# A decoder layer in fp32 on one core: eight modulation tiles moved into the up projection, the last pair's sums kept in SBUF, two blocks scaled by items of their own

## The chip, the core and the metric

The kernel runs on one core of one Trainium2 chip. The core has five engines that work side by side and wait for each other by semaphores: TensorE (PE, matmuls), VectorE (DVE), ScalarE (ACT), GpSimd (POOL) and SyncE (SP, which here only issues transfers). Sixteen DMA engines move data between the chip's memory (DRAM) and the on-chip memory SBUF; PE writes its results to PSUM. The metric is the time of one execution on the device in microseconds (us); a kernel's time is the median of its runs.

## The reference, cut to what matters

One decoder layer for 512 tokens of width 1024, all in fp32. A vector `c` is projected to six modulation vectors; two attention branches are gated, merged and projected; a gated MLP with a causal convolution of width 3 follows. Each half ends in a layer norm whose sum is scaled by a modulation vector.

```python
mod = c @ w_ada + b_ada                              # 6 x 1024
sh1, sc1, gt1, sh2, sc2, gt2 = split(mod, 6)
u = x * (1 + sc1) + sh1
...
merged = sigmoid(g_a) * (y_fox @ w_fox_proj) + sigmoid(g_b) * (y_sb @ w_sb_proj)
x = layer_norm(alpha * x + (1 + gt1) * (merged @ w_o), ln1_g, ln1_b)
u2 = x * (1 + sc2) + sh2
h = causal_depthwise_conv(u2 @ w_up, conv_w, conv_b)  # 5632 columns
h_gate, h_val = split(h, 2)
x = layer_norm(alpha * x + (1 + gt2) * ((silu(h_gate) * h_val) @ w_down), ln2_g, ln2_b)
```

`gt2`, the sixth vector, is needed last: it scales the output of the down projection.

## The kernel before

**Products.** Each fp32 product is made of three matmuls. A number is split into a high part (ACT copies it, rounded) and a low part (DVE subtracts, `lo_of`, L90); `mm3` (L130 to L133) and `product` (L1053 to L1055) then add high x high, high x low and low x high. So each tile of weights costs one ACT and one DVE operation before PE may use it: `wh` and `wl`.

**The ring of items.** All weights pass through one list, `items`. An item is a source and a routine that works on it. `weights(i)` loads up to item i + 5 on SP's queue into five buffers of 128x1024 (`raw`, 512 KB each) and runs the routines in the list's order. A buffer comes free when its item's routine has read it. The place of an item in the list therefore sets when it is loaded, and what it is loaded behind. SP's order is that of the list; on the other engines a scheduler sets the order.

**Modulation tiles.** The matrix of the modulation passes as 32 tiles of 128x1024 (`wa1`), beside some that are loaded ahead. Tiles 8 to 23 are for `sh2` and `sc2` (`mod_col`, one DVE operation of 128x1024 each, L194). Tiles 0 to 7 and 24 to 31 are for `gt1` and `gt2`: `ada_proc` (L566 to L580) multiplies each half by a column of `c` and adds it up in `ac`, two DVE operations per tile (L574 for a group's first, else L579). Four tiles make a group, g = 0, 1 for `gt1` and g = 6, 7 for `gt2`. `ada_split` splits a group's sum in high and low part, and `ada_sum` adds over the partitions with two matmuls against ones and puts the result into half of `gt[i]` (L600). Tiles 0 to 31 are put in the list by `add_ada`, behind projections, values and gates of the attention.

**The gates.** From about 296 to 345 us PE runs the gates of branch A (tiles of `in_wct`), the branch's projection and the merge. POOL adds the two branches (L731) and multiplies w_o's tiles by `gt1` (`wo_proc`, L625), DVE makes `ml` and `wl`. Then the output projection and the layer norm follow, up to 400.

**The up projection** runs over 44 tiles of `w_up` (n = 0 to 43), 24 matmuls of 512 columns each, from about 400 to 690; ACT and DVE do the convolution behind each tile (L1103 to L1105).

**The down projection** is in blocks of a 2 x 2 scheme with seven products (Winograd's form of Strassen's), whose weights come in 11 pairs p, each with four blocks of 512 columns: B11, B12, B22, B21. Per pair there are three items in the up projection's list: one raw item, to which POOL's queue adds a second load in memory (L156); B11, split; and `pair_proc` (L934 to L946). The last one makes two sums of blocks (L939, L940), splits them for the pair's early products, and stores for later, on ACT's queue, the raw item's two sums to `t13[p]` (L943) and B22 scaled by `gt2`, `wg` (L938), to `wgt[p]` (L944). Three of the seven products run early; the other four run after the up projection, in a phase each: phase Z (items `zi`: the right half of `t13`), W1 (`vi`: the left half of `t13`), X (`xi`: B21) and W (`wi`: `wgt`). Each of these items holds two pairs. `phase` (L1157) runs such a phase; `early_products` (L1059) runs the pairs' early products, that of the last pair, p = 10, inside phase Z. `tail` (L1142) does the layer norm by row blocks of 128 and sends them out.

## Time and profile before

| What | Value |
|---|---|
| Runs, us | 765.11, 768.05, 767.78 (median 767.78) |
| Profiled execution, us | 765.17 |
| Its span, first to last instruction, us | 763.4 |
| Mean granted clock of PE | 0.993 |
| DRAM read, written, MB | 117.07, 10.75 |

The profile is one execution. A row of a group gives the engine, the line, the operation, the tiles as out<-in, their shapes and a count; a row of the timeline starts with the start and the duration in us, and ends in brackets with the time that the engine stood idle before it and what ended that. "PEld" is the load of a matmul's stationary side, which runs beside PE. A duration of a matmul is longer than the step from one to the next, as they overlap in the array; 128x512 matmuls follow each other at 0.22 to 0.23 us.

### The profile page before, as it was taken

Reading aid. Unit: us, or ns where it says so; the run is one execution under the profiler, and the core shown is the slowest. Engines: PE = TensorE matmul, PEld = TensorE weight load, DVE = VectorE, ACT = ScalarE, POOL = GpSimd, SP = SyncE. Lnnn points to the kernel's source line nnn. Section 1 sums busy time; section 2 is a strip of 40 time slices with the busy share of each in tenths; the row PEclk is TensorE's granted clock in tenths of the full one; section 3 lists DMA queues with packets and bytes.
Section 4 is the critical chain, followed back from the end, with each engine's and each line's share of the span. In section 5 each row is a group of like instructions: output and inputs, shape, how many; then the busy total and the mean of one; then the engine's idle time right before and its main releaser. Section 6 shows DMA issues by size and latency. Waiting matters only on the chain.

```text
span 763.4 us, 9879 instructions
## 1 busy us (share of the span) xinstructions
PE 738.1 (97%) x3478; PEld 609.1 (80%) x3478; DVE 610.4 (80%) x1017; ACT 385.3 (50%) x678; POOL 107.0 (14%) x136
## 2 busy tenths in 40 slices
PE   8999999989989999899999999999999999999993
PEld 4878888877878888688889888888888888886783
DVE  6869799887699786975567989966786777768998
ACT  4567466684875664343046554443553355344630
POOL 1035223443000011363000000000000000000010
PEclk9999999999999999999999999999999999999998
DMA  9954556333344134552055576646754665555922
GB/s 334 406 186 133 170 173 214 110 112 112 114 135 139 66 128 143 175 185 78 5 190 147 166 229 193 190 156 190 263 171 161 222 192 151 169 186 159 321 81 78
DMA packets 43524, 128.54 MB, mean 168 GB/s; under 512 B 5681, under 2 KB 6193, under 8 KB 43474
## 3 DMA queue, kind: packets, MB, share of 16 engines
q1 hardware_dynamic: 37602, 112.09, 42.6%
q0 software_dynamic: 2416, 6.88, 5.0%
q10 hardware_dynamic: 3456, 8.93, 3.4%
q8 instruction: 27, 0.44, 0.2%
q14 instruction: 23, 0.19, 0.1%
HBM read 117.07 MB, written 10.75 MB: 167 GB/s over the span
## 4 chain that ended last, share of the span: by engine, by line
PE 73%; DVE 14%; DMA 5%; issue 4%; ACT 3%; SPq 1%; POOL 0%; DVEq 0%; ACTq 0%; POOLq 0%
PE ps L133 15%; PE ps L131 15%; PE ps L132 15%; PE ps L294 4%; PE ps L1054 4%; PE ps L1055 4%; PE ps L1053 4%; DVE wl L90 3%; DMA raw<-in_wa 2%; PE ps L887 2%; PE ps L886 2%; PE ps L888 2%; DVE om L506 2%; PE ps L527 1%; DVE raw L194 1%
## 5 line engine op out<-in xcount | busy, mean ns | idle before, releaser
L90 DVE TENSOR_TENSOR wl<-raw,wh 128x1024 fp32r<-128x1024 f32 (+2 forms) x114 | 136.1, 1194 | 60.2 <-ACT wh L176 60.0
L176 ACT ACTIVATE wh<-raw 128x1024 fp32r<-128x1024 f32 (+1 forms) x105 | 109.7, 1045 | 133.5 <-PE ps L132 90.4
L131 PE MATMUL ps<-u2h,wh 128*128 128x512 f32 (+1 forms) x376 | 141.5, 376 | 0.0
L133 PE MATMUL ps<-u2h,wl 128*128 128x512 f32 (+1 forms) x376 | 141.5, 376 | 0.0
L132 PE MATMUL ps<-u2l,wh 128*128 128x512 f32 (+1 forms) x376 | 141.4, 376 | 0.0
L133 PE MATMUL ps<-uh,wl 128*128 128x512 f32 x200 | 79.0, 395 | 2.7 <-DVE wl L90 2.7
L133 PEld LDWEIGHTS ps<-u2h,wl 128*128 128x128 f32 x376 | 70.8, 188 | 12.9
L131 PEld LDWEIGHTS ps<-u2h,wh 128*128 128x128 f32 x376 | 70.8, 188 | 12.8
L132 PEld LDWEIGHTS ps<-u2l,wh 128*128 128x128 f32 x376 | 70.8, 188 | 12.7
L131 PE MATMUL ps<-uh,wh 128*128 128x512 f32 x200 | 80.2, 401 | 0.0
L132 PE MATMUL ps<-ul,wh 128*128 128x512 f32 x200 | 78.9, 395 | 0.0
L156 POOL DMA_DIRECT2D raw<-in_wdp x11 | 9.5, 867 | 295.3 <-DVE raw L940 149.6
L133 PEld LDWEIGHTS ps<-uh,wl 128*128 128x128 f32 x200 | 37.9, 190 | 11.5 <-DVE wl L90 3.1
L507 POOL TENSOR_TENSOR pt<-pt,om 128x127 f32<-128x127 f32 (+3 forms) x32 | 42.7, 1347 | 9.4 <-DVE om L506 9.4
L131 PEld LDWEIGHTS ps<-uh,wh 128*128 128x128 f32 x200 | 38.0, 190 | 7.5
L132 PEld LDWEIGHTS ps<-ul,wh 128*128 128x128 f32 x200 | 38.1, 191 | 7.3
L1103 ACT ACTIVATE cv<-ps,cw 128x512 f32<-128x512 f32 x44 | 33.7, 766 | 16.8 <-PE ps L133 11.1
L1104 DVE SCALAR_TENSOR_TENSOR cv<-ps,cw,cv 128x511 f32<-128x511 f32 x44 | 32.8, 745 | 6.3 <-ACT cv L1103 6.3
L1111 ACT ACTIVATE cv<-cv 128x512 f32<-128x512 f32 x22 | 13.9, 632 | 41.7 <-DVE cv L1105 41.7
L1105 DVE SCALAR_TENSOR_TENSOR cv<-ps,cw,cv 128x510 f32<-128x510 f32 x44 | 32.7, 745 | 0.3
L625 POOL TENSOR_TENSOR raw<-raw,gt 128x1024 f32<-128x1024 f32 x8 | 20.5, 2567 | 69.7 <-DMA raw<-in_wo 58.2
L1054 PE MATMUL ps<-wl,hv 128*128 128x512 f32 x72 | 28.7, 398 | 1.4 <-DVE wl L90 1.4
(224 smaller groups left out, 1611.0 us busy)
## 6 DMA issues: line engine op xcount, KB each, us to landing
raw<-in_wup SPq DMA_DIRECT2D x44, 512.0 KB, 4.3
raw<-in_wa SPq DMA_DIRECT2D x32, 512.0 KB, 3.4
raw<-in_wct SPq DMA_DIRECT2D x25, 512.0 KB, 3.8
raw<-in_wdp SPq DMA_DIRECT2D x22, 512.0 KB, 5.6
wa<-in_wa SPq DMA_DIRECT2D x14, 512.0 KB, 7.7
raw<-in_wdp POOLq DMA_DIRECT2D x11, 512.0 KB, 7.2
raw<-in_wdp SPq DMA_DIRECT2D x22, 256.0 KB, 6.3
t<-raw ACTq DMA_DIRECT2D x11, 512.0 KB, 2.9
```

The costliest lines, as they stand in the source:

```text
L90: return V.tensor_tensor(o, i, fl(hi), ALU.subtract)
L131: PE.matmul(ps, wh, ah, start=first, stop=False)
L132: PE.matmul(ps, wh, al, start=False, stop=False)
L133: return PE.matmul(ps, wl, ah, start=False, stop=last)
L176: state["hi"] = S.activation(h[:, 0:cols], r[:, 0:cols], AF.Copy)
L294: PE.matmul(grp[g], w, u, start=j == 0 and n == 0, stop=j == KT - 1 and n == (1 if g == 7 else 2))
L507: G.tensor_tensor(pt[b][:, s : e - 1], pt[b][:, s : e - 1], om[:, s + 1 : e], ALU.mult)
L1053: PE.matmul(ps, ah, bh, start=first, stop=False)
L1054: PE.matmul(ps, ah, bl, start=False, stop=False)
L1103: S.activation(t, ps, AF.Identity, bias=cw[:, n, 3:4], scale=cw[:, n, 2:3])
L1104: V.scalar_tensor_tensor(t[:, 1:], ps[:, 0:511], cw[:, n, 1:2], t[:, 1:], ALU.mult, ALU.add)
L1105: V.scalar_tensor_tensor(t[:, 2:], ps[:, 0:510], cw[:, n, 0:1], t[:, 2:], ALU.mult, ALU.add)
```

## The change

Tiles 24 to 31 of the modulation leave the attention's part of the list and stand in that of the up projection, group 7 first. The two groups are split and summed apart. The last pair's sums are neither stored nor loaded; they are split in SBUF, so `t13` has ten tiles, and phases Z and W1 have five items and a last pair without one. Pairs 0 and 1 make no `wg`; their B22 is loaded a second time by an item of its own, scaled in place and stored by POOL's queue. The late items of `wgt` are put elsewhere in X's list.

```diff
+GTILES = (3, 5, 7, 8, 12, 16, 20, 24)
...
-            elif adas[0] < 32:
+            elif adas[0] < 24:
...
             add_bproj(1, j, lambda m, j=j: ma.__setitem__(j, m))
-            if j >= 3:
-                add_ada()
...
     for j in range(KT):
         add_bproj(0, j, merge(j))
-        add_ada()
...
-    add_ada(32 - adas[0])
+    add_ada(24 - adas[0])
...
     def pair_proc(p):
         def f(r):
             b = items[pi[p][0]][4]
-            g = z(F32, "wg")
-            V.tensor_tensor(g, r[:, 0:512], gt[1][:, 512:1024], ALU.mult)
+            if p > 1:
+                g = z(F32, "wg")
+                V.tensor_tensor(g, r[:, 0:512], gt[1][:, 512:1024], ALU.mult)
...
             with tc.issue_after(state["last"].ins):
-                S.dma_start(t13[p], b)
-                S.dma_start(wgt[p], g)
+                if p < FP - 1:
+                    S.dma_start(t13[p], b)
+                if p > 1:
+                    S.dma_start(wgt[p], g)
+            if p == FP - 1:
+                state["t13"] = wdc_proc(b)
             return w
         return f

-    wui, pi = [], []
+    def scale_proc(p):
+        def f(r):
+            V.tensor_tensor(r[:, 0:512], r[:, 0:512], gt[1][:, 512:1024], ALU.mult)
+            G.dma_start(wgt[p], r[:, 0:512])
+        return f
...
     for n in range(2 * FT):
         wui.append(add_item(wup[n], split_proc))
+        if n in GTILES:
+            k = GTILES.index(n)
+            wai[(10, 28)[k // 4]] = add_item(wa1[(28, 24)[k // 4] + k % 4], ada_proc((28, 24)[k // 4] + k % 4))
+        if n in (17, 21):
+            add_item(wdp[n // 4 - 4][:, 1024:1536], scale_proc(n // 4 - 4))
...
-    for p in range(0, FP, 2):
-        add_two(zi, lambda q: t13[q][:, 512:1024], p, FP)
+    for p in range(0, FP - 1, 2):
+        add_two(zi, lambda q: t13[q][:, 512:1024], p, FP - 1)
...
-        if p < 8:
+        if p < 10:
             add_late()
...
-            if n == 3:
-                for g in (6, 7):
-                    list(ada_split(g, 0))
-            if n == 4:
-                for g in (6, 7):
-                    list(ada_sum(g))
+            if n in (10, 28):
+                list(ada_split(7 if n == 10 else 6, wai[n]))
+            if n in (11, 30):
+                list(ada_sum(7 if n == 11 else 6))
...
-    def phase(ps, idx, end, take, mark):
+    def phase(ps, idx, end, take, mark, last=None):
...
+        if end < FP:
+            t = take(end)
+            for i in range(2):
+                product(ps[i], t[:, top[i]], t[:, bot[i]], *[v[last] for v in state["t13"]], False, True)
+            mark(len(idx))
```

How this moves instructions is seen in three places. The first is DVE at the gates, about 307 to 322 us. `sg` is a gate times a projection, `ml` the merged rows' low part, `wol` the low part of a tile of w_o, `ac` group 7's sum. Before:

```order
L90 TENSOR_TENSOR ml_3094<-sg_2919,mh_3093 128x512
L574 TENSOR_SCALAR ac_618_3108<-raw_3066,cTs 128x512
L579 SCALAR_TENSOR_TENSOR ac_618_3108<-raw_3066,cTs,ac_618_3108 128x512
L579 SCALAR_TENSOR_TENSOR ac_618_3108<-raw_3098,cTs,ac_618_3108 128x512 x2
L90 TENSOR_TENSOR wl_3183<-raw_3161,wh_3182 128x1024
L579 SCALAR_TENSOR_TENSOR ac_618_3108<-raw_3159,cTs,ac_618_3108 128x512
L619 TENSOR_TENSOR sg_2972<-ps_3139,sg_2972 128x512
L579 SCALAR_TENSOR_TENSOR ac_618_3108<-raw_3159,cTs,ac_618_3108 128x512
L579 SCALAR_TENSOR_TENSOR ac_618_3108<-raw_3163,cTs,ac_618_3108 128x512
L90 TENSOR_TENSOR ml_3155<-sg_2972,mh_3154 128x512
L579 SCALAR_TENSOR_TENSOR ac_618_3108<-raw_3163,cTs,ac_618_3108 128x512
L90 TENSOR_TENSOR wl_3254<-raw_3213,wh_3253 128x1024
```

The last row is the `wl` of 320.88. The same stretch with the change:

```order
L91 TENSOR_TENSOR ml_3074<-sg_2897,mh_3073 128x512
L91 TENSOR_TENSOR wol_3087<-raw_3044,woh_3085 128x512
L91 TENSOR_TENSOR wol_3088<-raw_3044,woh_3086 128x512
L91 TENSOR_TENSOR wl_3152<-raw_3139,wh_3151 128x1024
L620 TENSOR_TENSOR sg_2950<-ps_3119,sg_2950 128x512
L91 TENSOR_TENSOR wl_3196<-raw_3143,wh_3195 128x1024
L91 TENSOR_TENSOR ml_3135<-sg_2950,mh_3134 128x512
L91 TENSOR_TENSOR wl_3232<-raw_3184,wh_3231 128x1024
```

No `ac` is left among them. The counterpart of the row of 320.88 is `wl_3196`; it now stands ahead of the second `ml`, and the next one, `wl_3232`, follows that `ml` at once.

The second place is SP's queue at the start of phase W1, whose first item is pairs 0 and 1 (`t_0`, `t_1`). Before:

```order
L153 DMA raw_6361<-t_8_70 128x512
L153 DMA raw_6361<-t_9_71 128x512
L153 DMA raw_6378<-t_10_72 128x512
L153 DMA raw_6410<-t_0_62 128x512
L153 DMA raw_6410<-t_1_63 128x512
```

With the change:

```order
L154 DMA raw_6362<-t_8_70 128x512
L154 DMA raw_6362<-t_9_71 128x512
L154 DMA raw_6386<-t_0_62 128x512
L154 DMA raw_6386<-t_1_63 128x512
L154 DMA raw_6419<-t_2_64 128x512
```

The load of `t_10` is gone. DVE, at the same place, works on pair 10's sums as follows (`raw_6255` holds them, `wdl` are their low parts):

```order
L938 TENSOR_TENSOR raw_6255<-raw_6255,raw_6217 128x512
L91 TENSOR_TENSOR wl_6460<-raw_6386,wh_6459 128x1024
L939 TENSOR_TENSOR raw_6255<-raw_6255 128x512
L91 TENSOR_TENSOR wdl_6371<-raw_6255,wdh_6369 128x512
L91 TENSOR_TENSOR wl_6490<-raw_6419,wh_6489 128x1024
L91 TENSOR_TENSOR wdl_6372<-raw_6255,wdh_6370 128x512
L91 TENSOR_TENSOR wdl_6380<-raw_6217,wdh_6378 128x512
L91 TENSOR_TENSOR wdl_6381<-raw_6217,wdh_6379 128x512
```

Before, the two sums and the two `wdl` of `raw_6254` stood in a row, without a `wl` between them; `wl_6460` and `wl_6490` are W1's first two items.

The third place is DVE early in the up projection (n = 1 to 4), where there is now an `ac` of group 7 between the convolution's operations (`cv`):

```order
L575 TENSOR_SCALAR ac_758_4051<-raw_3841,cTs 128x512
L1124 TENSOR_TENSOR cv_3982<-cv_3982,cv_4010 128x512
L1116 SCALAR_TENSOR_TENSOR cv_4040<-ps_3849,cw,cv_4040 128x511
L580 SCALAR_TENSOR_TENSOR ac_758_4051<-raw_3841,cTs,ac_758_4051 128x512
L1117 SCALAR_TENSOR_TENSOR cv_4040<-ps_3849,cw,cv_4040 128x510
L91 TENSOR_TENSOR wl_4059<-raw_3932,wh_4058 128x1024
L580 SCALAR_TENSOR_TENSOR ac_758_4051<-raw_4045,cTs,ac_758_4051 128x512
L1048 TENSOR_TENSOR sg_764_4092<-cv_3982 128x256
L580 SCALAR_TENSOR_TENSOR ac_758_4051<-raw_4045,cTs,ac_758_4051 128x512
```

Before, this stretch held no `ac`, and `acl` and the sums of both groups stood behind the tile n = 4. At the very end PE's order changes as well: before, its last four matmuls are of the second piece of 256 columns of row block 3; with the change both pieces of block 3 are done first, and 24 matmuls of 512 columns of block 2 are last.

More of the change, by code (lines that the diff above doesn't have):

```diff
@@ L56, in layer_kernel @@
     cons = ctx.enter_context(tc.tile_pool(name="cons", bufs=1))
-    t13 = [tc.dram_tile([P, 1024], F32, name=f"t13_{p}") for p in range(FP)]
+    t13 = [tc.dram_tile([P, 1024], F32, name=f"t13_{p}") for p in range(FP - 1)]
     wgt = [tc.dram_tile([P, 512], F32, name=f"wgt_{q}") for q in range(FP)]
@@ L942, in f @@
             with tc.issue_after(state["last"].ins):
-                S.dma_start(t13[p], b)
-                S.dma_start(wgt[p], g)
-            return w
-        return f
-    wui, pi = [], []
+                if p < FP - 1:
[4 more added lines that the diff above has]
+                state["t13"] = wdc_proc(b)
+            return w
+        return f
+    def scale_proc(p):
[3 more added lines that the diff above has]
+        return f
+    wui, pi, wai = [], [], {}
     def add_pair_items(p):
@@ L978, in layer_kernel @@
             add_pair_sums(FP - 1)
-    for p in range(0, FP, 2):
-        add_two(vi, lambda q: t13[q][:, 0:512], p, FP)
+    for p in range(0, FP - 1, 2):
+        add_two(vi, lambda q: t13[q][:, 0:512], p, FP - 1)
         if p > 2:
@@ L1220, in layer_kernel @@
     Z = [bank() for _ in range(2)]
-    phase(Z, zi, FP, g_part(0), z_mark)
+    phase(Z, zi, FP - 1, g_part(0), z_mark, 1)
     W1 = [bank() for _ in range(2)]
-    phase(W1, vi, FP, g_part(1), v_mark)
+    phase(W1, vi, FP - 1, g_part(1), v_mark, 0)
     X = [bank() for _ in range(2)]
```

## The prediction

> **What bounds the kernel now.** I read the page's busy times first, then the chain of waits, then windows of 20 us, and then the waits of TensorE (PE) where a window falls short.

> ```profile
> PE 738.1 (97%) x3478; PEld 609.1 (80%) x3478; DVE 610.4 (80%) x1017; ACT 385.3 (50%) x678; POOL 107.0 (14%) x136
> PE 73%; DVE 14%; DMA 5%; issue 4%; ACT 3%; SPq 1%; POOL 0%; DVEq 0%; ACTq 0%; POOLq 0%
> ```

> PE is busy 738.1 of 763.4 us, and the chain is PE for 73%. The change removes no matmul, so all there is to win are the 25.3 us in which PE stands, and matmuls at a low clock. Windows show where these are (columns: length; busy us and instructions of PE, PEld, DVE, ACT, POOL; granted clock; DMA share; GB/s).

> ```profile
> 140.00:160.00 20.00, 17.93 (x89) 14.79 (x87) 16.71 (x23) 13.98 (x25) 9.52 (x13) 1.00 0.36 116
> 200.00:220.00 20.00, 17.43 (x94) 14.43 (x93) 16.49 (x32) 12.83 (x29) 2.06 (x4) 1.00 0.41 132
> 320.00:340.00 20.00, 17.85 (x71) 14.58 (x72) 14.91 (x15) 7.25 (x10) 9.84 (x5) 0.91 0.66 215
> 420.00:440.00 20.00, 20.00 (x90) 16.55 (x89) 18.81 (x30) 11.67 (x21) 0.00 (x0) 1.00 0.55 175
> 440.00:460.00 20.00, 20.00 (x90) 16.58 (x89) 17.56 (x31) 9.43 (x15) 0.87 (x1) 1.00 0.69 214
> 460.00:480.00 20.00, 20.00 (x90) 16.31 (x89) 19.37 (x32) 9.25 (x16) 0.86 (x1) 1.00 0.63 190
> 700.00:720.00 20.00, 18.20 (x75) 13.47 (x74) 18.43 (x26) 11.77 (x18) 0.00 (x0) 1.00 0.95 306
> ```

> In the up projection (400 to 680) PE stands nowhere: 90 matmuls per 20 us, 0.222 us each. The losses lie in the attention (140 to 220), whose orders the change leaves as they are up to about 215 us; at 320, in the gates; at 700, in the phases Z and W1 of the down projection; and in the tail.

> ```profile
> 322.15 0.50 PE L133 MATMUL ps<-uh,wl 128*128 128x512 f32 x1 [2.72 <-DVE wl L90]
> 322.00:324.00 2.00, 1.85 (x6) 1.53 (x7) 2.00 (x5) 0.34 (x1) 0.00 (x0) 0.75 0.86 260
> 324.00:326.00 2.00, 2.00 (x6) 1.52 (x6) 1.75 (x2) 0.83 (x2) 1.27 (x1) 0.50 0.98 375
> 325.47 0.63 PE L133 MATMUL ps<-uh,wl 128*128 128x512 f32 x1
> 325.89 0.63 PE L131 MATMUL ps<-uh,wh 128*128 128x512 f32 x1
> ```

> One wait of PE at the gates takes 2.72 us, and behind it the granted clock falls to 0.50: matmuls follow each other at 0.42 us (325.47, 325.89) where 0.23 is usual, eight of them, so 8 x 0.2 = 1.6 us more. That place loses 2.72 + 1.6 = 4.3 us.

> **The change part by part: the gates.** Why is this `wl` late?

> ```profile
> 311.01 0.75 DVE L579 SCALAR_TENSOR_TENSOR ac<-raw,cTs,ac 128x512 f32<-128x512 f32 x1
> 314.87 2.68 DVE L90 TENSOR_TENSOR ml<-sg,mh 128x512 fp32r<-128x512 f32 x1
> 317.47 2.89 DVE L579 SCALAR_TENSOR_TENSOR ac<-raw,cTs,ac 128x512 f32<-128x512 f32 x1
> 320.88 1.21 DVE L90 TENSOR_TENSOR wl<-raw,wh 128x1024 fp32r<-128x1024 f32 x1
> 317.33 2.47 POOL L625 TENSOR_TENSOR raw<-raw,gt 128x1024 f32<-128x1024 f32 x1 [0.34 <-ACT wh L176]
> 315.98 1.06 ACT L176 ACTIVATE wh<-raw 128x1024 fp32r<-128x1024 f32 x1 [0.63 <-DMA raw<-in_wct]
> ```

> Its `wh` was done at 317.04, and PE wanted `wl` at 319.4. In between DVE did one `ac` operation of a modulation tile for 2.89 us, while POOL multiplied a tile of w_o. Usually it takes 0.75 (row at 311.01). Ahead of it the load itself came late (ACT waited for it), since tiles 24 to 31 took their turns in the ring of five raw buffers. The change takes out all eight tiles here: eight loads of 512 KB and 16 operations on DVE. Without the 2.89 alone, `wl` would end at about 319.2; without the other loads it also starts some us earlier. So the stall goes, and with it the clock's fall: 4.3 us. The bounds are 0 (another operation takes its place, a rival below) and 4.3, as a stall can't be won twice; I take 4.3, because what stands in front of `wl` is removed in both of its causes.

> [...]

> **The up projection.** It takes on eight loads of 512 KB (at n = 3, 5, 7, 8, 12, 16, 20, 24), two reloads of 256 KB (n = 17, 21) with two stores by POOL's queue, and on DVE 2 x 0.48 + 14 x 0.75 = 11.5 us; the scaling of two blocks replaces two `wg` of equal length.

> ```profile
> L574 DVE TENSOR_SCALAR ac<-raw,cTs x4: 468/482/1054, 66.8 to 307.1; 128x512 f32<-128x512 f32 x4
> 422.13 1.29 DVE L90 TENSOR_TENSOR acl<-ac,ach 128x512 fp32r<-128x512 f32 x2
> 429.44 1.29 DVE L600 SCALAR_TENSOR_TENSOR gt<-ps,gt 128x512 f32<-128x512 f32 x2 [0.26 <-PE ps L598]
> 434.37 0.69 DVE L938 TENSOR_TENSOR wg<-raw,gt 128x512 f32<-128x512 f32 x1
> DVE wl L90 <- ACT wh L176: 60.0, 38, 4.6
> L176 ACT ACTIVATE wh<-raw 128x1024 fp32r<-128x1024 f32 (+1 forms) x105 | 109.7, 1045 | 133.5 <-PE ps L132 90.4
> ```

> The tight place is 420 to 480. DVE is busy 18.81 + 17.56 + 19.37 = 55.74 there and idle 4.26. Added by four tiles are 0.48 + 7 x 0.75 = 5.7; half of `acl` and of the sums (0.65 each) moves to n = 28 and 30, and `wg` goes (0.69): net 3.7. That fits in 4.26, without room. What covers it beyond this is that weights are split ahead: DVE waited 60.0 us for `wh`, 38 times, and ACT 90.4 us for PE to be done with a buffer, so a split lies ready and waits for PE; lateness must eat that lead first. Later windows have 14 of 20 busy and take the other four tiles easily. I take 0; without that cover the price is what DVE lacks, 0 to 5.7 us, and below 0 it can't be, as PE has no idle time here to give.

> **Phases Z and W1.** Pair 10's sums are stored to DRAM and loaded again:

> ```profile
> 694.43 0.69 DVE L940 TENSOR_TENSOR raw<-raw 128x512 f32<-128x512 f32 x1
> 695.24 0.33 ACTq L943 DMA_DIRECT2D t<-raw  x1
> 703.02 1.06 ACT L176 ACTIVATE wh<-raw 128x1024 fp32r<-128x1024 f32 x1 [1.12 <-DMA raw<-t]
> 700.18 0.69 DVE L1184 TENSOR_TENSOR u<-p,ps 128x512 f32<-128x512 f32 x1 [1.86 <-ACT p L1182]
> 701.95 0.73 PE L1053 MATMUL ps<-wh,hv 128*128 128x512 f32 x2 [0.40 <-ACT wh L176]
> 705.58 0.50 PE L1054 MATMUL ps<-wl,hv 128*128 128x512 f32 x1 [0.71 <-DVE wl L90]
> 716.99 0.50 PE L1054 MATMUL ps<-wl,hv 128*128 128x512 f32 x1 [0.44 <-DVE wl L90]
> ```

> SP's queue holds the load of `t13[10]` in front of W1's, and it can't go before the store of 695.24 has landed; so W1's weights come late (ACT waits 1.12 us for `raw<-t` at 703), and PE stands 20 - 18.20 = 1.8 us between 700 and 720. The change drops store and load, and SP runs straight on to W1's. DVE's count stays: two splits of 128x512 from the sums replace those from the loads. Bounds: 1.8 if every stall goes; -1.0 if the splits of W1's first weights, which now stand in front of pair 10's own splits (695), hold up its early products by nearly one `wl` of 1.2. I take 1.1, since DVE is nearly as full as PE from 720 on.

> **The tail.** PE's order changes: row block 3's two pieces of 256 columns come first, and block 2's last products end it.

> ```profile
> 751.40 0.69 DVE L1253 TENSOR_TENSOR xn<-xn,ps 128x512 f32<-128x512 f32 x1 [0.38 <-PE ps L1055]
> 752.01 1.01 DVE L1254 BATCH_NORM_STATS2 st<-xn 128x6 f32<-128x256 f32 x2
> 752.94 0.40 DVE L1253 TENSOR_TENSOR xn<-xn,ps 128x256 f32<-128x256 f32 x1
> 758.70 1.53 DVE L1152 SCALAR_TENSOR_TENSOR xn<-xn,mv,ln 128x512 f32<-128x512 f32 x3
> ```

> From 751.40 to 760.23 DVE works without a pause, 8.83 us; an addition of 256 columns (0.40) and two statistics of 256 (0.4 each) of block 3 now precede PE's last product, about 0.9 less. Bounds 0 and 0.9 (DVE had only 0.38 us to spare in front of 751.40, but the 1.86 us that it waited at 700 are filled now); I take 0.9.

> **Sum.** 4.3 + 0 + 1.1 + 0.9 = 6.3 us off the profiled execution's 765.17 (span 763.4), 758.9. The runs shown are 765.11, 767.78, 768.05; what makes two of them 2.7 longer one trace can't tell. On the median: 767.78 - 6.3 = **761.5**.

> **Rivals.** *The stretch lands on the weights.* POOL's multiplications of w_o stay (317.33, 2.47 us), and `ml` at 314.87 took 2.68 beside one, so it isn't only `ac` that is drawn out. If the critical `wl` is, 2.1 us of stall come back and the low clock too: gain 0.6 + 2.0, time 765.2. Against it: its load comes earlier now, and two causes would have to be replaced by one. [...]

> *Slower: the ring runs late in the up projection.* A round of four tiles and early products is (96 + 18) x 0.222 = 25.3 us. It has 7 items before (4 tiles, 3 of a pair) and 8 now, 9 in the rounds with a scale item, so 3.6 us each becomes 2.8; five buffers give 14 us from a free buffer to the need.

> ```profile
> raw<-in_wdp SPq DMA_DIRECT2D x22, 512.0 KB, 5.6
> raw<-in_wdp POOLq DMA_DIRECT2D x11, 512.0 KB, 7.2
> ```

> A pair's first item needs 5.6 and then 7.2 by POOL's queue, 12.8 us, now behind the scale's store on that queue. From 1.2 us more, pairs are late, and PE stands in early products. With 2.7 us in each of five rounds: 13.5 - 6.3 = 7.2 slower, 775.0. For it: DMA share 0.63 to 0.69 before anything is added. Against it: a pair's sums are needed only a round later.

> *Pair 10's splits are late* (-1.0 for 1.1): 763.6. *The low clock hangs on something else and stays*: 767.78 - 2.7 - 2.0 = 763.1. For it: in 140 to 160 and 200 to 220 PE stood 2.1 and 2.6 us, and the clock stayed at 1.00; against it: here it falls right behind the wait.

> **How the numbers follow.** Forecast 0.60, stretch on the weights 0.14, ring late 0.12, pair 10 late 0.08, clock stays 0.06. About 0.5% (3.9 us: 763.9 and 771.7) is what can be told from no change. Faster: 0.60 and the last two, less what run spread of 2.7 pushes across, 0.70; same 0.18; slower 0.12. The range reaches down to the fastest run's basis with all of Z (765.11 - 6.3 - 0.7 = 758.1, less 1) and up to the first rival with the spread of the runs: 757 to 768.5, which leaves out the ring's case.

> **What would show it.** Right: no PE wait above 1 us between 300 and 345 and clock 1.00 there; 90 matmuls per 20 us from 420 to 680; no ACT wait for `raw<-t` near 703; under 8.3 us from PE's last matmul to DVE's end. Wrong: any PE wait in the up projection, or a stretched `wl` beside POOL at the gates.

## The result, and the profile after

| | Before | Changed |
|---|---|---|
| Median of 19 runs, us | 767.21 | 764.49 |
| Lowest, highest | 764.93, 769.70 | 762.07, 767.72 |
| Profiled execution, us | 765.17 | 765.29 |
| Its span, us | 763.4 | 763.5 |

The ratio of the changed kernel's runs to those of before is 0.9968, with a 95% interval from 0.9955 to 0.9981: about 2.5 us faster, where 6.3 were forecast. The direction was right and the range (757 to 768.5) held the median, though a range that wide holds the kernel before as well; the size was not right: less than half of the forecast came.

The two profiled executions are equally long, although the medians differ by 2.7. So the first reading of the changed kernel's profile is by windows of 20 us (columns as in the prediction):

```profile
200.00:220.00 20.00, 17.16 (x77) 13.97 (x76) 15.14 (x30) 11.20 (x27) 1.83 (x4) 0.85 0.34 107
320.00:340.00 20.00, 20.00 (x90) 16.57 (x89) 13.04 (x12) 8.63 (x14) 11.59 (x6) 1.00 0.43 138
460.00:480.00 20.00, 20.00 (x90) 16.54 (x89) 20.00 (x35) 7.62 (x12) 0.86 (x1) 1.00 0.77 229
520.00:540.00 20.00, 19.03 (x84) 15.49 (x83) 13.10 (x21) 9.38 (x17) 0.58 (x1) 1.00 0.74 234
540.00:560.00 20.00, 18.42 (x77) 14.05 (x77) 15.90 (x27) 7.57 (x13) 0.85 (x1) 1.00 0.85 273
680.00:700.00 20.00, 19.54 (x84) 15.29 (x83) 16.68 (x25) 11.45 (x18) 0.00 (x0) 1.00 0.47 147
700.00:720.00 20.00, 19.93 (x88) 16.15 (x88) 19.33 (x31) 11.56 (x20) 0.00 (x0) 1.00 0.78 255
```

In the kernel before, the two windows in the middle of the up projection were:

```profile
520.00:540.00 20.00, 20.00 (x90) 16.56 (x89) 13.38 (x21) 7.41 (x12) 0.01 (x1) 1.00 0.48 168
540.00:560.00 20.00, 20.00 (x90) 16.55 (x89) 13.66 (x23) 9.34 (x17) 0.85 (x1) 1.00 0.80 263
```

Four things are to be seen. At 320 PE now does 90 matmuls at full clock, where it did 71. At 700 it stands 0.07 us instead of 1.80. But from 520 to 560, in the middle of the up projection, it lost 19 of 180 matmuls; before, there was no loss at all. And at 200, where the change does nothing, the clock fell to 0.85 in this execution and not in the one of before.

To put numbers on the places, I lined up both traces by the count of PE's matmuls: how much later or earlier the k-th one starts than before.

```
k-th matmul   before, us   changed minus before, us
        960       210.2     -0.39
       1020       224.1     +2.67    attention: clock at 0.50 after a wait that both have
       1500       317.9     +2.67
       1560       336.2     -1.98    gates: -4.65
       2500       530.5     -2.10
       2640       562.2     +1.85    up projection, n = 21 to 24: +3.95
       3180       684.9     +1.89
  DVE's end       760.2     -0.1     phases and tail: -2.0
```

So the change took 4.65 us at the gates and 2.0 us from phase Z to the end, as forecast, and gave 3.95 back in the up projection, which wasn't. The +3.06 between 960 and 1020 is not the change's: the same 60 matmuls take 13.97 us in the profile of before and 17.03 here, but 15.41 in a second profile of the changed kernel and 17.40 in the control below, which has the orders of before. The clock goes with it: the mean of the window from 200 to 220 us is 1.00 before and 0.85 here, 0.91 in that second profile and 0.89 in the control. Without it the sum is -4.65 - 2.0 + 3.95 = -2.7, and -3.1 with some 0.4 of small drifts; the medians show -2.7.

What PE waited for in the up projection (its timeline, rows with a wait, and its list of waits):

```profile
537.24 0.47 PE L132 MATMUL ps<-u2h,wh 128*128 128x512 f32 x1 [0.97 <-DVE cv L1117]
543.20 0.47 PE L132 MATMUL ps<-u2h,wh 128*128 128x512 f32 x1 [0.27 <-DVE cv L1117]
551.20 0.50 PE L1067 MATMUL ps<-wdh,fh 128*128 128x512 f32 x1 [0.92 <-ACT wdh L641]
```

```profile
PE ps L132 <- DVE cv L1117: 1.4, 3, 1.0
```

At 537.24 and 543.20 tiles n = 22 and 23 begin. They do not wait for their weights: the split of tile 22 ended at 531.06. They wait for a PSUM bank (the place where a tile's sums are collected), that is for the convolution's last addition (L1117) of the tile two before, which reads that tile's sums. ACT's timeline shows why that was late:

```profile
528.74 1.06 ACT L177 ACTIVATE wh<-raw 128x1024 fp32r<-128x1024 f32 x1 [5.71 <-DMA raw<-in_wup]
533.12 1.06 ACT L177 ACTIVATE wh<-raw 128x1024 fp32r<-128x1024 f32 x1 [2.80 <-DMA raw<-in_wup]
534.09 0.76 ACT L1115 ACTIVATE cv<-ps,cw 128x512 f32<-128x512 f32 x1
549.57 1.06 ACT L1112 ACTIVATE ln<-ln 128x1024 f32<-128x1024 f32 x1 [5.77 <-DMA ln<-in_lnrow]
550.54 1.13 ACT L641 ACTIVATE wdh<-raw 128x512 fp32r<-128x512 f32 x2
```

In this trace ACT did not pass over a split that waited for its load. The splits of tiles ahead (22 at 528.74, 23 at 533.12) stand in front of a finished tile's convolution (L1115). The loads for these splits came late, ACT stood 5.71 and 2.80 us in front of them, and tile n = 20, which PE finished at 530.8, got its convolution only at 534.09, behind tile 23's split. Further on ACT waits 5.77 us for a row of the layer norm, with the split of pair 4's sums (`wdh`) behind it, for which PE waits at 551.20.

The tail, DVE's last run without a pause (compare 751.40 and 758.70 before):

```profile
752.17 0.69 DVE L1270 TENSOR_TENSOR xn<-xn,ps 128x512 f32<-128x512 f32 x1 [1.42 <-PE ps L1069]
758.62 1.53 DVE L1164 SCALAR_TENSOR_TENSOR xn<-xn,mv,ln 128x512 f32<-128x512 f32 x3
```

From 752.17 to 760.15 are 7.98 us, where it was 8.83. But before, that run began ahead of PE's last product, which ended at 751.83; now it ended at 752.13. From there to DVE's end are 8.40 us before and 8.02 now, 0.4 less.

### The profile page after: what moved, and what is told of

Its sections match the earlier page's. It is cut to its first block, busy times and chain, and to the rows that moved or that the text cites. A ratio compares the mean times of both kernels' runs of the same rounds, so it can differ in the third digit from the quotient of the medians.

```text
span 763.5 us, 9879 instructions
## 1 busy us (share of the span) xinstructions
PE 739.0 (97%) x3478; PEld 609.9 (80%) x3478; DVE 604.4 (79%) x1017; ACT 385.0 (50%) x678; POOL 108.3 (14%) x138
## 4 chain that ended last, share of the span: by engine, by line
PE 68%; DVE 17%; DMA 8%; issue 3%; ACT 3%; SPq 0%; ACTq 0%; DVEq 0%
PE ps L132 14%; PE ps L133 14%; PE ps L134 14%; PE ps L295 5%; DVE wl L91 4%; DMA raw<-in_wa 3%; PE ps L1068 2%; PE ps L1069 2%; PE ps L886 2%; PE ps L884 2%; PE ps L885 2%; PE ps L1067 2%; DVE om L507 2%; PE ps L546 1%; PE ps L528 1%
## 5 line engine op out<-in xcount | busy, mean ns | idle before, releaser
L132 PE MATMUL ps<-u2h,wh 128*128 128x512 f32 (+1 forms) x376 | 141.7, 377 | 1.4 <-DVE cv L1117 1.4
L133 PE MATMUL ps<-u2l,wh 128*128 128x512 f32 (+1 forms) x376 | 141.2, 376 | 0.0
L132 PEld LDWEIGHTS ps<-u2h,wh 128*128 128x128 f32 x376 | 70.8, 188 | 15.4 <-issue 2.6
L133 PEld LDWEIGHTS ps<-u2l,wh 128*128 128x128 f32 x376 | 70.8, 188 | 12.6
L132 PE MATMUL ps<-uh,wh 128*128 128x512 f32 x200 | 80.2, 401 | 0.0
L133 PE MATMUL ps<-ul,wh 128*128 128x512 f32 x200 | 78.8, 394 | 0.0
L132 PEld LDWEIGHTS ps<-uh,wh 128*128 128x128 f32 x200 | 38.0, 190 | 7.5
L133 PEld LDWEIGHTS ps<-ul,wh 128*128 128x128 f32 x200 | 38.1, 190 | 7.3
L1115 ACT ACTIVATE cv<-ps,cw 128x512 f32<-128x512 f32 x44 | 33.5, 767 | 16.1 <-PE ps L134 11.0
L1117 DVE SCALAR_TENSOR_TENSOR cv<-ps,cw,cv 128x510 f32<-128x510 f32 x44 | 32.6, 745 | 0.2
L195 DVE SCALAR_TENSOR_TENSOR raw<-raw,cbc 128x1024 f32<-128x1024 f32 x16 | 21.0, 1314 | 11.4 <-DMA raw<-in_wa 11.3
## 6 DMA issues: line engine op xcount, KB each, us to landing
raw<-in_wup SPq DMA_DIRECT2D x44, 512.0 KB, 4.8
raw<-in_wa SPq DMA_DIRECT2D x32, 512.0 KB, 3.4
raw<-in_wct SPq DMA_DIRECT2D x25, 512.0 KB, 3.3
raw<-in_wdp SPq DMA_DIRECT2D x22, 512.0 KB, 5.7
wa<-in_wa SPq DMA_DIRECT2D x14, 512.0 KB, 7.9
raw<-in_wdp POOLq DMA_DIRECT2D x11, 512.0 KB, 7.8
t<-raw ACTq DMA_DIRECT2D x10, 512.0 KB, 4.2
```

Source lines behind the costliest of these rows:

```text
L132: PE.matmul(ps, wh, ah, start=first, stop=False)
L133: PE.matmul(ps, wh, al, start=False, stop=False)
L195: return V.scalar_tensor_tensor(wt[:, c], wt[:, c], 1.0, cbc[:, c], ALU.mult, ALU.mult, accum_out=o)
L1115: S.activation(t, ps, AF.Identity, bias=cw[:, n, 3:4], scale=cw[:, n, 2:3])
L1117: V.scalar_tensor_tensor(t[:, 2:], ps[:, 0:510], cw[:, n, 0:1], t[:, 2:], ALU.mult, ALU.add)
```

## The experiments

The measure of the loss is the time from the 2500th to the 2640th matmul, about n = 20 to 24. These 140 matmuls take 31.73 us at full speed, as before; the changed kernel took 35.68, and 34.41 in a second profile (at the end), so differences of about 1 us between single profiles say little. Ratios are to the kernel before.

**Is a buffer held too long?** (A) The scale items' buffer is free only when POOL's store has landed (the second item's, in the changed kernel, at 526.06, and SP issues a load at 526.08); loads behind it wait. The first kernel scales into a tile of its own.

```diff
     def scale_proc(p):
         def f(r):
-            V.tensor_tensor(r[:, 0:512], r[:, 0:512], gt[1][:, 512:1024], ALU.mult)
-            G.dma_start(wgt[p], r[:, 0:512])
+            g = z(F32, "wg")
+            V.tensor_tensor(g, r[:, 0:512], gt[1][:, 512:1024], ALU.mult)
+            G.dma_start(wgt[p], g)
```

> The changed kernel, but the two scaled blocks go into a tile of their own, from which POOL's queue stores them, so the ring's buffer is free after one DVE operation of 0.69 us instead of after the store's landing (issued 520.28, landed 526.06). ACT's order is the same as in the changed kernel. Theory A (the buffer that is held by the store makes the up projection's loads late): PE's waits for the convolution's second addition between 520 and 546 (1.4 us in three waits) go, and the loss against before from tile n = 20 to 24 (3.95 us) falls to about 2. Theory B (the added modulation tiles make the ring and the DMA engines late): 3.95 stays within 0.5. Theory C (ACT waits for the layer norm's row): the wait in the early products at 551 stays in any case.

Measured: 36.29 us, no less than 35.68; ratio 0.9977 (0.9963 to 0.9992). PE's wait at n = 22, in this kernel's timeline, is even longer:

```profile
537.48 0.47 PE L132 MATMUL ps<-u2h,wh 128*128 128x512 f32 x1 [1.67 <-DVE cv L1118]
```

This run doesn't test theory A, since the buffer did not come free early. DVE's multiplication of the second item ran only at 531.77, where the changed kernel has it at 519.29 (the first row is of this kernel, the second of the changed one):

```profile
531.77 0.69 DVE L954 TENSOR_TENSOR wg<-raw,gt 128x512 f32<-128x512 f32 x1
519.29 0.69 DVE L953 TENSOR_TENSOR raw<-raw,gt 128x512 f32<-128x512 f32 x1
```

So the buffer was held until 532.46, longer than by the store (526.06), and SP's load at 532.48 went right behind it. What the store holds up is seen in the changed kernel's trace, on SP's queue:

```profile
522.00 0.33 SPq L154 DMA_DIRECT2D raw<-in_wup  x1
526.08 0.33 SPq L154 DMA_DIRECT2D raw<-in_wdp  x1
526.74 4.67 SPq L154 DMA_DIRECT2D raw<-in_wup  x2
```

The load at 526.08, the pair's last item, goes right behind the store's landing. But tile 23's, the first of the two at 526.74, goes right behind another landing, that of pair 3's own store to `t13` (issued at 520.62, landed at 526.68; before, 513.75 and 516.85). A shorter hold by the scale item alone would not have let tile 23's load go sooner, by this reading; no run shows it.

**The layer norm's row** (C).

```diff
-        if n == 24:
+        if n == 34:
             for i in range(2):
                 lnr2.append(...)
                 nc.sync.dma_start(lnr2[i], ...)
-        if n == 28:
+        if n == 38:
             S.activation(lnr2[0], lnr2[0], AF.Copy, scale=-0.5)
```

> The changed kernel, but the layer norm's two rows are loaded behind tile n = 34 and scaled behind n = 38 instead of 24 and 28. Theory C (ACT waits 5.77 us for the row at 549.57 with the split of pair 4's sums queued behind it): PE's wait for wdh at 551 and those right behind it go, about 2.2 us of the 3.95 between n = 20 and n = 24, and 1.7 stay. Theories A and B alone: 3.95 stays, since the sums themselves are late.

Measured: 33.59 us, 2.1 less; ratio 0.9944 (0.9918 to 0.9971). The list of PE's waits has none for `wdh` any more, and the first wait stays:

```profile
PE ps L132 <- DVE cv L1117: 1.3, 2, 0.9
```

So the 3.95 are two losses of about equal size: 1.8 by the tiles' late loads and 2.1 by the row in front of pair 4's split. In the second profile of the changed kernel the first is 1.5 and the second 1.1, by the count of matmuls.

**Group 6's tiles out of the way** (B).

```diff
-GTILES = (3, 5, 7, 8, 12, 16, 20, 24)
+GTILES = (3, 5, 7, 8, 26, 30, 34, 38)
```

> The changed kernel, but group 6's four modulation tiles stand at n = 26, 30, 34, 38 and its split and sum at n = 40 and 42 instead of 28 and 30. Theory B (tiles at 12, 16, 20, 24 make the ring late): the 3.95 us between n = 20 and 24 go to under 1. Theory A: the scale items alone still hold a buffer 14 us, about 1.7 us stay. Where the tiles go to, loads have room (rounds of 8 items, DMA share 0.45 to 0.7 before), 0 to 1 us.

Measured: 31.73 us, the whole loss is gone, although the scale items stayed where they were. But the kernel is slower than before, 1.0021 (1.0005 to 1.0038). The loss only moved. The list of PE's waits of this kernel:

```profile
PE ps L132 <- DVE cv L1117: 2.5, 2, 1.5
PE ps L132 <- DVE gt L601: 1.1, 1, 1.1
PE ps L1067 <- ACT hv L88: 1.0, 1, 1.0
```

The longest of the first kind is at 563.92 in the timeline, about n = 26 (1.7 us by the count of matmuls), the other at 473.76 (1.2 us). The other two kinds are at the group's sum, which now comes at the end of the up projection, just ahead of phase Z (3.7 us). "Loads have room there" was wrong.

**The last pair alone**, on the kernel before (`pair_proc` without the store of pair 10's sums, which are split from SBUF, and phases Z and W1 as in the change).

> The kernel before with one part of the change alone: the last pair's sums are split from SBUF and neither stored nor loaded. My sum: about 2.0 us off (1.1 in phases Z and W1, 0.9 in the tail), and no wait of ACT for t13's loads near 703. Rival (DVE is as full as PE from 720 on): PE's waits go but DVE ends no earlier, under 0.5 us. In the gates and in the up projection nothing changes against before.

Measured: ratio 0.9967 (0.9953 to 0.9981), span 761.7 against 763.4: 1.7 us, of which 0.1 was there before phase Z. The windows of this kernel at the gates and in phase W1:

```profile
320.00:340.00 20.00, 17.96 (x72) 14.65 (x73) 13.04 (x14) 6.53 (x10) 10.26 (x6) 0.91 0.58 203
700.00:720.00 20.00, 20.00 (x90) 16.52 (x89) 19.19 (x31) 11.19 (x16) 0.00 (x0) 1.00 0.77 253
```

The gates are as before, phase W1 is without a wait. This one part alone is worth as much as the whole change.

**The scale items out of the way**, group 6's tiles where the change has them.

```diff
-        if n in (17, 21):
-            add_item(wdp[n // 4 - 4][:, 1024:1536], scale_proc(n // 4 - 4))
+        if n in (33, 37):
+            add_item(wdp[n // 4 - 8][:, 1024:1536], scale_proc(n // 4 - 8))
```

> The changed kernel, but the two scale items stand at n = 33 and 37 instead of 17 and 21, in rounds without a modulation tile, so no round has nine items. Theory B1 (nine items a round are too many for the ring, whatever they are): the waits of PE for the convolution's second addition at n = 22 and 23 (1.4 us, with what hangs on them 1.8 of the 3.95) go, as they did when group 6's tiles were moved. Theory B2 (group 6's tiles of 512 KB are it, the scale items count for little): 1.8 stays within 0.5. The wait for the layer norm's row at n = 23 (2.2 us) may stay in either.

Measured: 32.05 us, so 3.6 of the 3.95 are gone, PE's wait behind the row with them; ratio 0.9925 (0.9912 to 0.9938), median 761.03. The up projection's windows of this kernel:

```profile
520.00:540.00 20.00, 20.00 (x90) 16.57 (x89) 14.97 (x24) 9.75 (x17) 0.00 (x0) 1.00 0.56 182
540.00:560.00 20.00, 19.97 (x88) 16.21 (x88) 13.24 (x23) 8.01 (x11) 0.86 (x1) 1.00 0.78 256
```

With the third kernel this shows that neither the tiles of group 6 nor the scale items alone make the loss at n = 20 to 24, but both in the same rounds. B2 falls; whether any ninth item would do, as B1 says, is asked below.

**Both at once**: the row and the scale items moved.

> The changed kernel with both: the layer norm's rows loaded behind n = 34 and scaled behind n = 38, the scale items at n = 33 and 37. If the two causes add, nothing of the 3.95 us between n = 20 and 24 is left, and the kernel is 4.65 + 2.0 + 0.3 - 0.3 = 6.5 us, 0.8 to 0.9%, under the kernel before. If the scale items cost as much where they go to, 1 to 2 us less than that.

Measured: 31.73 us, nothing left at n = 20 to 24; but ratio 0.9936 (0.9917 to 0.9954), no better than moving the scale items alone: 4.75 us off where 6.5 were expected, which fits the second case that was named. By the count of matmuls 2.0 us are lost between the 2900th and the 3000th. In the timeline PE waits at a new place, where the row's loads (behind n = 34) and the scale items (33, 37) now meet:

```profile
619.87 0.47 PE L132 MATMUL ps<-u2h,wh 128*128 128x512 f32 x1 [0.72 <-DVE cv L1117]
641.24 0.47 PE L132 MATMUL ps<-u2h,wh 128*128 128x512 f32 x1 [0.72 <-DVE cv L1117]
```

**The gates alone**, on the kernel before.

```diff
-            elif adas[0] < 32:
+            elif adas[0] < 24:
...
-            if n == 3:
-                for g in (6, 7):
-                    list(ada_split(g, 0))
             if n == 4:
-                for g in (6, 7):
-                    list(ada_sum(g))
+                gt[1] = gt_tile(1)
```

> The kernel before without modulation tiles 24 to 31: they are neither loaded nor multiplied nor summed, so the second gate is its bias alone; nothing else is changed. If the tiles are the cause of the wait at the gates, the 2.7 us wait and the low clock behind it go, 4.3 to 4.7 us from 320 to 336, and the up projection stays without a wait; with four matmuls of the sums gone 0.9 us more. If another cause (POOL's multiplications of w_o stretching the weights' split) makes the wait, half of it or more stays.

Measured: from the 1500th to the 1560th matmul 13.60 us, where before takes 18.25; no wait at the gates and none in the up projection. Ratio 0.9950 (0.9922 to 0.9977).

```profile
320.00:340.00 20.00, 20.00 (x90) 16.57 (x89) 12.19 (x11) 9.27 (x15) 10.67 (x6) 1.00 0.43 143
```

The tiles were the cause of that wait, and POOL's multiplications, which are all still there, don't bring it back. Whether it was the tiles' loads or their operations on DVE, this run doesn't part.

**A control**: the kernel before with the row's loads moved.

> The kernel before with the layer norm's rows loaded behind n = 34 and scaled behind n = 38. A control: before, ACT waits 4.57 us for the row as well, but with pair 4's splits already done, and PE waits nowhere; so 0 within 0.3 us in the profile's up projection. If this alone is faster by over 1 us, the row's load costs something that PE's waits don't show.

Measured: ratio 0.9998 (0.9986 to 1.0010), 31.73 us. The row costs only where a late split stands behind it. This profile showed one thing more, on the clock; it is told at the end.

**A turn in the ring, or bytes?** Scale items at 33 and 37, and at 17 and 21 dummies:

```diff
+        if n in (17, 21):
+            add_item(wdp[n // 4 - 4][:, 1024:1032], small_proc)
+    def small_proc(r):
+        V.tensor_copy(sc, r[:, 0:8])
```

> The kernel with the scale items at n = 33 and 37, plus two dummy items at n = 17 and 21 that load 8 columns (4 KB) and copy them, with no store. They take a turn in the ring, and move almost no bytes; ACT's order up to about 570 us is that of the changed kernel. Theory S (a ninth item's turn in the ring and the order that follows from it): the 3.95 us between n = 20 and 24 come back, within 1. Theory M (its 256 KB of load and 256 KB of store keep the DMA engines from the tiles): under 1 us comes back.

Measured: 33.23 us, 1.5 over full speed, where the same kernel without the dummies has 0.3 (32.05). ACT waits again for the tiles' loads and for the row:

```profile
527.05 1.06 ACT L177 ACTIVATE wh<-raw 128x1024 fp32r<-128x1024 f32 x1 [4.80 <-DMA raw<-in_wup]
546.85 1.06 ACT L1119 ACTIVATE ln<-ln 128x1024 f32<-128x1024 f32 x1 [4.48 <-DMA ln<-in_lnrow]
```

Between the two theories' numbers: the turn, and the order of instructions that follows from it, makes about 1.2. Another 1.2 to 2.45, by which of the changed kernel's two profiles it is compared with, come with what the items do themselves (bytes, a store that holds the buffer, a multiplication, which this run doesn't part). So B1's "whatever they are" is not shown. Ratio 0.9926 (0.9905 to 0.9947).

**A sixth buffer** (`LOADS = 6`, `NZ = 56`).

> The changed kernel with six raw buffers instead of five (and 56 instead of 58 tiles of 128x512 for all else, as memory is full). Theory S: a sixth buffer gives each load one item's time (2.8 us) more, so at least 3 of the 3.95 us between n = 20 and 24 go. Theory M: DMA's share there is 0.74 to 0.85, a sixth buffer doesn't change it, and 2 us or more stay. Two tiles fewer may cost elsewhere, which would be seen outside n = 20 to 24.

Measured: 31.73 us, the whole loss gone, with DMA's share at 0.60 and 0.74 in the two windows. But other losses came: 3.2 us at the end of the up projection, as here,

```profile
660.00:680.00 20.00, 17.53 (x74) 13.40 (x74) 13.19 (x20) 7.62 (x14) 0.00 (x0) 1.00 0.65 197
```

and less gain in phase Z and the tail. Ratio 0.9964 (0.9951 to 0.9977). It moves much of the order elsewhere, so it speaks for the ring, without being a clean proof.

**The better kernel and the change side by side**, on one chip.

> The kernel with the scale items at n = 33 and 37 once more, in five rounds on one chip beside the changed kernel: if the 3.95 us of the up projection are what the changed kernel lacks against the forecast, this one is 0.6 to 0.9% under the kernel before, near the 761.5 us of the sum, and about 0.4 to 0.5% under the changed kernel.

> The changed kernel itself, as the other side of that comparison: 0.2 to 0.45% under the kernel before, with the waits at n = 22 to 24 (about 3.95 us) in its profile again, whatever the clock does in the attention.

Measured: 761.76 us with the scale items late, ratio 0.9933 (0.9914 to 0.9953), 31.96 us for the 140 matmuls; 764.36 for the change, 0.9975 (0.9961 to 0.9990), 34.41 us. The first beats both kernels, by 5.0 and 2.6 us (0.66 and 0.34%; against the change 0.4 to 0.5% were expected). The changed kernel's loss came again, but as 2.7 us, not 3.95.

## Why the forecast's size was wrong

**The gates: right.** The wait is gone and the clock is 1.00 there. The term was 4.3; by the count of matmuls it is 4.65 where the clock fell before. It is not always so: in the control the same wait cost 16.64 - 13.60 = 3.0 us, as the clock stayed. So 4.3 was the price of one execution; of the three profiles that have this wait two show 4.7 and one 3.0, and the mean over runs is not known. The rival by which the low clock hangs on something else was half right: behind the control's wait, 2.73 us long, the clock stayed at 1.00. The rival of the stretch that lands on the weights didn't come; without the tiles POOL's multiplications made no wait at all.

**Phases Z and W1 and the tail: right in the sum.** PE stood 0.46 + 0.07 us from 680 to 720, and 0.11 + 1.80 before: 1.4 against a term of 1.1. From the 3180th matmul to PE's last end it is 1.6 us less than before (65.36 for 66.96), and from there to DVE's end 0.4 less, against 0.9. So the 2.0 at the end are 1.6 + 0.4, where the sum had 1.1 + 0.9: that they agree is in part luck. The tail's 0.9 was the change of DVE's last run (8.83 to 7.98), which before began ahead of PE's end.

**The up projection: here the prediction failed.** Its step was "I take 0", on two grounds; its own sign of being wrong, a wait of PE in this stage, is there (0.97 us at 537.24). The first, that DVE has room for 3.7 us between 420 and 480, held in its outcome: PE lost nothing there. DVE was 18.18, 17.96 and 20.00 busy, 0.4 more than before in all where 3.7 were reckoned, and 2.5 more from 480 to 520, so part of its work lay later. The second was that "a split lies ready and waits for PE; lateness must eat that lead first". That measured the wrong margin. At n = 22 the split was ready 6.2 us ahead (531.06 to 537.24) and PE waited all the same, since ACT and DVE had stood in front of that split and the next with a finished tile's convolution behind them, and PE wants its PSUM bank back. What a late load has to eat is not the split's lead over PE, but the time until the next evacuation (the operation that reads a finished tile's sums, so that its bank comes free) behind it in the same queue. In place of 0 the step costs 3.95 us in one profile and 2.7 in the other.

The rival of the late ring had the place right (rounds of nine items), but its size and sign wrong; its price of 13.5 assumed five rounds at 2.7, a number for which it gave no source, and its reason, the pair's first item behind the scale's store on POOL's queue, was not it: the loss came in the second of the two rounds with nine items, and there the pair's load left POOL's queue at 518.12, ahead of the store at 520.28. The row of the layer norm wasn't thought of. It was in the trace of before, a wait of 4.57 us that no one stood behind; the change put pair 4's split behind it.

With the up projection's term put right, 6.3 - 3.95 = 2.35 by the first profile and 3.6 by the second; the runs show 2.4 to 2.7. With most of its cause removed the kernel takes 761.0 and 761.8, where the sum said 761.5. That is closer than the sum deserves: it started from 767.78, the median of three runs, and the gains beside the kernel before are 5.9 and 5.0 us, not 6.3.

## What to carry to other kernels

When work moves under a stage that seems to have cover, don't measure the cover at the bound engine's operands alone: look at what stands behind each waiting instruction on the engines that feed it, since an operation for later that waits for a load holds up an evacuation for now (here tile 20's, from 530.8 to 534.09). Count items per round where a ring of buffers feeds the stage: an item costs its turn (about 1.2 us here) as well as what it moves and holds, and moving two of them by 16 tiles was worth as much as the whole change had been (2.6 us beside 2.4). Look in the trace whether an experiment did what it was made for: the first one here was meant to free a buffer early and freed it late. And line up two traces by the count of the bound engine's instructions before reading spans: two equal spans here hid four differences.

## What the runs showed of the hardware

**The clock's fall is not tied to the length of a wait alone.** Three waits of PE behind the first 100 us of the kernel before are 2 to 3 us long, of 2.71, 2.57 and 2.72 us; they end at 160.63, 214.83 and 322.15. At the gates, before, the clock fell to 0.50 behind 2.72 us. In the control the wait was as long, and the clock stayed (timeline and windows of the control):

```profile
326.01 0.50 PE L133 MATMUL ps<-uh,wl 128*128 128x512 f32 x1 [2.73 <-DVE wl L90]
```

```profile
326.00:328.00 2.00, 1.99 (x9) 1.65 (x10) 2.00 (x4) 0.57 (x1) 0.00 (x0) 1.00 0.68 217
```

At 212 us, in the attention, which the change leaves alone, the clock stayed at 1.00 behind a wait of 2.57 us before, and fell to 0.50 in the changed kernel, where the wait is 2.83 (timelines of before and of the changed kernel, then windows of 2 us of the latter):

```profile
214.83 0.39 PE L469 MATMUL ps<-m,s 68*128 68x256 f32 x1 [2.57 <-DVE m L90]
214.70 0.58 PE L470 MATMUL ps<-m,s 68*128 68x256 f32 x1 [2.83 <-DVE m L91]
```

```profile
214.00:216.00 2.00, 1.30 (x5) 1.21 (x6) 1.94 (x4) 0.00 (x0) 0.00 (x0) 0.50 0.45 125
218.00:220.00 2.00, 2.00 (x6) 1.52 (x6) 1.97 (x4) 0.85 (x4) 0.77 (x2) 0.50 0.03 4
```

In ten of the thirteen profiles of this study with five buffers the clock between 200 and 220 us was below 1.00, with 0.85 to 0.92 as the mean of the window. From the 700th to the 1020th matmul (about 155 to 224 us), a stretch in which the two programs hardly differ, the profile of before takes 69.10 us and the changed kernel's first one 72.0. The runs of one kernel spread by about 5 us (764.93 to 769.70 before), and part of that goes with the clock: of the 74 runs of the kernel before that were made beside the experiments, the 23 with a mean granted clock of 0.991 or more have a median of 766.1 us, the 27 with 0.988 or less one of 767.9.
